# Projections of 128 tokens over 512 columns in one pass, with queries kept unscaled in DRAM

## The chip, the cores and the metric

The kernel runs on one core of one Trainium2 chip. The metric is the device time of one execution in microseconds (us). The kernel before takes 1717.66 us, the median of three runs that lie between 1717.14 and 1718.26 us.

Engine names in what follows: PE is TensorE (matrix products, also transposes), DVE is VectorE, ACT is ScalarE, POOL is GpSimd, SP is SyncE, whose queue issues every DMA transfer here. Each engine runs its instructions in the order in which they stand in its own queue.

## The reference

One layer of a decoder on 1024 tokens of width 1024, all in float32. Cut to what matters here:

```python
xn = rms_norm(x, norm_mix)
proj = xn @ w_in
q_nsa, kv_nsa, g_nsa, conv_in, q_mem, g_merge = split(proj, [512, 768, 24, 1024, 512, 3072])
# A: sparse attention, 8 heads of 64 in 2 groups
q = rms_norm(heads(q_nsa), nsa_qk_norm[0])
k_c, v_c, k_s, v_s, k_w, v_w = split(kv_nsa, 6)       # compressed, selected, window
ks, kw = rms_norm(k_s, nsa_qk_norm[2]), rms_norm(k_w, nsa_qk_norm[3])
br_nsa = nsa_attention(q, kc, vc, ks, vs, kw, vw, sigmoid(g_nsa)) @ w_nsa_out
# B: gated convolution of width 31 per channel, LayerNorm over the 512 channels, silu
a, ag = split(conv_in, 2)
br_conv = silu(layer_norm(causal_conv31(a * sigmoid(ag)) + conv_b)) @ w_conv_out
# C: cross attention, 4 heads of 128, into 256 memory tokens
qm = rms_norm(heads(q_mem), mem_qk_norm[0]); km = rms_norm(..., mem_qk_norm[1])
br_mem = (softmax(qm @ km.T * 128 ** -0.5) @ vm) @ w_mem_out
# merge and feed forward
gm = sigmoid(g_merge)
h = x + (gm[0] * br_nsa + gm[1] * br_conv + gm[2] * br_mem) @ w_out
out = h + (silu(hn @ w_gate) * (hn @ w_up)) @ w_down     # hn = rms_norm(h, norm_ffn)
```

## The kernel before

**Products.** A float32 factor is split into a high part, which PE takes in a fast 32-bit format, and the rest (`split`, line 130: a cast on ACT, a subtraction on DVE). A product is then three matmuls, high by high, high by low, low by high (`mm3`, line 151). Almost all work of PE goes through `mm` at line 144.

**Normalised tokens.** `norm_x` (line 246) takes 256 tokens of x at a time. ACT squares and sums each row (L204), takes the root (L136), DVE inverts it and scales the row (L208), PE transposes it in 128x128 pieces (L229), ACT scales the pieces by the gain into the high part (L220), DVE makes the low part (L221). Both halves of the 1024 tokens stay in SBUF as eight tiles (`XN`).

**Projections that are laid out by token** (`tok_proj`, line 279) make 128 tokens by 256 columns in one PSUM bank half: 8 steps of depth times 3 matmuls of 256 columns; two such tiles fill a bank. Their weights come as two loads of 512 rows by 256 columns (`row_units`, line 269). They are run for the queries of the cross attention (columns from `C_QM`, two passes), the queries of the sparse attention (from `C_Q`, two passes), and the selected and window keys and values (from `C_KV`, two passes), besides four passes over the memory tokens. `raw_proj` (line 324) copies queries from PSUM to SBUF; `head_norms` (line 308) later squares, sums, scales them in place. The queries stay in four SBUF tiles (`QMQ[0]`, `QMQ[1]`, `Q[0]`, `Q[1]`).

**Order of the program:** x is normalised along with the first pass of cross-attention queries (lines 337 to 346); then the convolution's input projections, gates, compressed keys and values, memory keys and values; then cross attention (`mem_attention`, line 569) for two pairs of heads, each along a further pass of queries; the last pass of queries; the tail of the convolution (lines 613 to 635: two sums over channels by `ones` matmuls, square, root, reciprocal, silu); the keys and values (lines 638 to 662); then sparse attention.

**Taps.** The 31 taps of the convolution for four channel tiles, 124 DVE instructions of about 1.3 us (lines 373, 374), are spread by hand over the products between the first projection and the last query (lines 598 to 605).

**Sparse attention** is a list of 80 units: for each of 8 token tiles and each of 2 groups one compressed, two selected and two window units. `scores(u)` runs four units ahead of `values(u)`. I call the five units of one token tile and group a group of units; each begins with a transpose of the queries at line 688.

**Filler.** The merge gates' projection (line 801 on) has 24 weight tiles, each with two halves of 24 matmuls of 512 columns. It has the lowest priority (`FILL`) and its own single PSUM bank `pf`; each half ends in an ACT copy (L814) to `fz` and a DMA to `zd`. The scheduler puts it wherever it expects PE to have nothing else. The first 12 tiles (`N_EARLY`), 24 halves, may stand anywhere; each step of the later ones must stand behind a certain unit of the attention.

**What sets the order.** A scheduler orders the instructions of each engine once, before the run, by priority and by when it expects their inputs. On the chip the order is fixed.

## Time and profile before

| | |
|---|---|
| median of three runs | 1717.66 us |
| the profiled execution, its own time | 1716.36 us |
| span of its trace | 1714.6 us |
| PE busy | 1692.3 us (99% of the span) |
| DVE busy | 1065.6 us (62%) |
| ACT busy | 731.3 us (43%) |
| POOL busy | 515.2 us (30%) |
| mean granted TensorE clock | 0.999 |

The stages lie in the trace thus: the first queries and the normalisation of x to 57 us, the convolution's projections and compressed keys to 190 us, memory tokens and cross attention to 370 us, queries, keys and the convolution's tail to 443 us, sparse attention to 850 us, then branch projections, merge and feed forward. "Busy" says that a matmul was somewhere in PE, not that PE ran at its peak: how close it is, the distance from one matmul's start to the next one's tells.

### The profile page before, as it was taken

How to read it: one execution, taken by the hardware profiler on the slowest of the kernel's cores; microseconds unless marked ns; L12 is line 12 of the kernel's file. 1: busy time of each engine (PE TensorE's matmuls, PEld its weight loads, DVE VectorE, ACT ScalarE, POOL GpSimd, SP SyncE). 2: the span in 40 equal slices, each digit the busy share in tenths (PEclk: the TensorE clock that was granted, in tenths of full speed). 3: DMA queues.
4: the chain of work that ended last, by engine and by line, in shares of the span. 5: the costliest groups of instructions: out<-in, count | busy, mean ns of one | idle time of the engine just before them, and what ended most of it. 6: DMA issues, size and time to landing. Idle time of an engine off the chain costs nothing.

```text
span 1714.6 us, 24413 instructions
## 1 busy us (share of the span) xinstructions
PE 1692.3 (99%) x9096; PEld 1457.9 (85%) x9096; DVE 1065.6 (62%) x1825; ACT 731.3 (43%) x1370; POOL 515.2 (30%) x478
## 2 busy tenths in 40 slices
PE   7999999999999999999999999999999999999999
PEld 7887998999888889999888888788888888888887
DVE  5599997876355566666654625856545554466665
ACT  6312544444466656666653424533222222233332
POOL 0000011200145434444204501375555777310000
PEclk9999999999999999999999999999999999999999
DMA  6112433112122111111385223233333445793763
GB/s 213 50 40 74 160 93 99 38 56 75 50 67 64 57 38 56 47 34 45 127 290 197 98 80 117 77 113 106 110 99 123 145 163 166 270 393 135 224 236 123
DMA packets 174173, 203.51 MB, mean 119 GB/s; under 512 B 10772, under 2 KB 117572, under 8 KB 173030
## 3 DMA queue, kind: packets, MB, share of 16 engines
q1 hardware_dynamic: 174054, 201.95, 35.4%
q8 instruction: 71, 1.16, 0.3%
q14 instruction: 48, 0.39, 0.1%
HBM read 151.58 MB, written 50.33 MB: 118 GB/s over the span
## 4 chain that ended last, share of the span: by engine, by line
PE 93%; DVE 3%; ACT 2%; issue 1%; DMA 1%; POOL 0%; SPq 0%; DVEq 0%; ACTq 0%; POOLq 0%
PE ps L144 57%; PE pf L144 19%; PE ps L1158 11%; PE ps L762 3%; PE pf L1158 1%; DVE slab L132 1%; PE ps L688 0%; PE ps L229 0%; PE ps L746 0%; DMA st<-in_w_in_dram 0%; PE ps L552 0%; DVE wsl L132 0%; ACT slab L131 0%; ACT slab L220 0%; DVE t L128 0%
## 5 line engine op out<-in xcount | busy, mean ns | idle before, releaser
L144 PE MATMUL ps<-slab,wsl 128*128 128x512 f32 (+1 forms) x1664 | 370.3, 381 | 1.4 <-ACT slab L131 0.9
L144 PEld LDWEIGHTS ps<-slab,wsl 128*128 128x128 f32 x1664 | 301.9, 188 | 61.5 <-ACT slab L131 1.2
L144 PE MATMUL pf<-slab,fsl 128*128 128x512 f32 x1236 | 323.1, 399 | 4.2 <-ACT fz L814 1.7
L144 PEld LDWEIGHTS pf<-slab,fsl 128*128 128x128 f32 x1236 | 222.9, 188 | 45.7 <-ACT fz L814 3.1
L144 PE MATMUL ps<-wsl,slab 128*128 128x256 f32 (+1 forms) x1512 | 221.1, 299 | 3.5 <-ACT slab L220 1.5
L144 PEld LDWEIGHTS ps<-wsl,slab 128*128 128x128 f32 x1512 | 199.5, 192 | 14.7 <-DVE slab L221 3.3
L1054 DVE TENSOR_TENSOR t<-ps,t 128x512 f32<-128x512 f32 x127 | 86.9, 688 | 108.0 <-PE ps L144 106.8
L374 DVE SCALAR_TENSOR_TENSOR slab<-slab,cw 128x1021 f32<-128x1021 f32 (+16 forms) x120 | 151.6, 1270 | 1.7
L144 PE MATMUL ps<-slab,fsl 128*128 128x512 f32 x636 | 147.8, 389 | 0.0
L144 PEld LDWEIGHTS ps<-slab,fsl 128*128 128x128 f32 x636 | 119.4, 188 | 24.9
L132 DVE TENSOR_TENSOR t<-ps,t 128x512 fp32r<-128x512 f32 (+2 forms) x192 | 117.2, 630 | 25.5 <-ACT t L131 23.9
L1158 PE MATMUL ps<-wsl 128*128 128x512 f32 x495 | 118.5, 389 | 0.0
L144 PE MATMUL ps<-t,slab 128*128 128x256 f32 x624 | 115.3, 292 | 0.9 <-DVE t L132 0.8
L132 DVE TENSOR_TENSOR wsl<-st,wsl 128x1024 fp32r<-128x1024 f32 x64 | 83.0, 1297 | 50.6 <-ACT wsl L131 47.5
L542 POOL TENSOR_SCALAR t<-t,sm 128x256 f32<-128x256 f32 x32 | 25.4, 810 | 286.2 <-DVE sm L538 286.2
L1158 PEld LDWEIGHTS ps<-wsl 128*128 128x128 f32 x495 | 92.9, 188 | 19.3
L131 ACT CAST wsl<-st 128x1024 fp32r<-128x1024 f32 x65 | 68.3, 1051 | 91.8 <-PE ps L144 50.6
L131 ACT CAST t<-ps 128x512 fp32r<-128x512 f32 (+2 forms) x192 | 97.5, 539 | 20.2 <-PE ps L762 18.4
L144 PEld LDWEIGHTS ps<-t,slab 128*128 128x128 f32 x624 | 93.6, 189 | 6.3 <-DVE t L132 1.0
L144 PE MATMUL ps<-slab,qt 128*128 128x384 f32 (+3 forms) x384 | 94.7, 338 | 0.0
L131 ACT CAST wsl<-t 128x1024 fp32r<-128x1024 f32 x42 | 44.2, 1054 | 97.6 <-POOL t L128 43.3
L676 POOL TENSOR_SCALAR wsl<-wsl,sm,gsb 128x640 f32<-128x640 f32 (+7 forms) x76 | 59.7, 795 | 77.7 <-DVE sm L671 67.2
(238 smaller groups left out, 2698.4 us busy)
## 6 DMA issues: line engine op xcount, KB each, us to landing
t<-in_w_down_dram SPq DMA_DIRECT2D x70, 256.0 KB, 4.2
fst<-in_w_in_dram SPq DMA_DIRECT2D x24, 512.0 KB, 3.6
zd<-fz SPq DMA_DIRECT2D x48, 256.0 KB, 2.0
t<-zd SPq DMA_DIRECT2D x24, 512.0 KB, 4.0
st<-in_w_in_dram SPq DMA_DIRECT2D x22, 512.0 KB, 3.6
st<-in_w_gate_dram SPq DMA_DIRECT2D x22, 512.0 KB, 4.4
st<-in_w_up_dram SPq DMA_DIRECT2D x22, 512.0 KB, 4.1
ad<-t SPq DMA_DIRECT2D x44, 256.0 KB, 3.3
```

The source lines that it names most:

```text
L131: m = nc.scalar.copy(hi, src)
L132: return m, (eng or nc.vector).tensor_tensor(lo, src, hi.bitcast(F32), op=OP.subtract)
L144: m = nc.tensor.matmul(o, a, b, start=start, stop=stop)
L374: return nc.vector.scalar_tensor_tensor(acc[:, s:], u[:, :S - s], cw[:, ct, 30 - s:31 - s], acc[:, s:], op0=OP.mult, op1=OP.add)
L542: nc.gpsimd.tensor_scalar(pm[:, tt, h, :], pm[:, tt, h, :], rec[:, j:j + 1], 1.0, op0=OP.mult, op1=OP.mult)
L676: nc.gpsimd.tensor_scalar(tiles[h], tiles[h], rec[:, h:h + 1], gsb[:, i, c0:c0 + 1], op0=OP.mult, op1=OP.mult)
L762: nc.tensor.transpose(b[:, j - j0, h, :], tiles[h][:, j * P:(j + 1) * P], ident)
L1054: nc.vector.tensor_tensor(o, a_, b_, op=OP.add)
L1158: nc.tensor.matmul(B[t], a_, b_, start=start and k == 0 and j == 0, stop=k == FH - 1 and j == 2, skip_group_check=True)
```

## The change

1. Queries, selected and window keys and values are projected 512 columns at a time (`wide_proj`, `wide_unit`): 128 tokens in one PSUM bank, weights as four loads of 256 rows by 512 columns.
2. All four heads of cross-attention queries are now made in the first stage, and all sparse-attention queries along the two rounds of cross attention; the keys and values follow.
3. Queries are copied from PSUM and sent to a DRAM buffer `qraw` as they are; only their sums of squares stay (`rqm`, `rqn`). `mem_qT` and `load_q` read them back and scale them.
4. The keys stand ahead of the code that spreads the taps, so that the taps are spread over the keys too, and the tail of the convolution comes behind the keys.

```diff
+    def wide_unit(w, c0, u, st=None, alloc=wslab):
+        if st is None:
+            st = stage.tile([P, 2, 512], F32, tag="st", name=nm("st"))
+        nc.sync.dma_start(st, w[u * 256:(u + 1) * 256, c0:c0 + 512].rearrange("(k p) c -> p k c", p=P))
...
+        split(w_[0], w_[1], st)
+        return w_
+    def wide_proj(ws, t):
+        o = bank([512])
+        half, a = t // 4, (t % 4) * P
+        for k in range(KT):
+            hi, lo = ws[k // 2]
+            mm3(o, xn(0, k, half, a, a + P), xn(1, k, half, a, a + P), hi[:, k % 2, :], lo[:, k % 2, :], k == 0, k == KT - 1)
+        return o
+    def queries(ws, t, j, stat):
+        h = stat.shape[2]
+        ps = wide_proj(ws, t)
+        raw, sq = t2([512]), t2([h, 512 // h])
+        nc.scalar.copy(raw, ps)
+        nc.sync.dma_start(qraw[j, t], raw)
+        nc.scalar.activation(sq, ps.rearrange("p (h d) -> p h d", h=h), AF.Square)
+        nc.vector.tensor_reduce(stat[:, t, :], sq, axis=AX.X, op=OP.add)
...
-    ws = row_units(w_in, C_QM)
+    ws = [wide_unit(w_in, C_QM, u, alloc=slab) for u in range(2)]
     xin += [rows2(x, tp * 256) for tp in range(1, 4)]
+    norm_x(0)
+    ws += [wide_unit(w_in, C_QM, u, t4([2, 512]), slab) for u in range(2, 4)]
...
+    for t in range(NT):
+        queries(ws, t, 0, rqm)
+        if t % 2 == 0 and t < NT - 2:
+            norm_x(t // 2 + 1)
+    stat_rms(rqm)
...
     def mem_qT(hp, tp):
-        qn = QMQ[hp][:, 2 * tp:2 * tp + 2]
+        qn = t2([2, 2, P])
+        nc.sync.dma_start(qn.rearrange("p t h d -> p t (h d)"),
+                          qraw[0, 2 * tp:2 * tp + 2, :, hp * 256:(hp + 1) * 256].rearrange("t p c -> p t c"))
+        nc.vector.tensor_tensor(qn, qn, rqm[...].to_broadcast([P, 2, 2, P]), op=OP.mult)
+        gain_mul(qn, gm[:, 0, :])
...
-                raw_proj(ws, tp, dest)
+                queries(ws, 4 * hp + tp, 1, rqn)
...
+    ws = [wide_unit(w_in, C_Q, u, alloc=slab if u == 3 else wslab) for u in range(4)]
+    mem_attention(0, ws)
+    pm3 = mem_attention(1, ws)
+    stat_rms(rqn)
+    KSW = [slab([2, S]) for _ in range(2)]
+    VSW = [slab([NT, 2, P]) for _ in range(2)]
+    ws = [wide_unit(w_in, C_KV, u, alloc=t4 if u == 3 else wslab) for u in range(4)]
...
+    for t in range(NT):
+        v = wide_proj(ws, t).rearrange("p (s a g d) -> p s a g d", s=2, a=2, g=2)
...
     with low(TAP):
         along = products[first_tap:]
...
+    def load_q(i):
+        QN[i] = t2([8, 64])
+        nc.sync.dma_start(QN[i].rearrange("p h d -> p (h d)"), qraw[1, i])
+        nc.vector.tensor_tensor(QN[i], QN[i], rqn[:, i, :, None].to_broadcast([P, 8, 64]), op=OP.mult)
```

**Where instructions stand now, on two engines' queues.** Of two names joined by an arrow the left is written; `slab_140` and `slab_143` are tokens 0 to 255 of x, `slab_159` and `slab_162` tokens 256 to 511, `ps` a PSUM bank, `pf` the filler's, `wsl`, `fsl` and `st` weights.

ACT in the first stage of the kernel before, from the first high parts of x on:

```order
L220 ACTIVATE slab_169<-ps_189,gcol 128x256
L220 ACTIVATE slab_170<-ps_198,gcol 128x256
L204 ACTIVATE t_31_252,sm_251<-slab_159 128x1024
L220 ACTIVATE slab_171<-ps_207,gcol 128x256
L220 ACTIVATE slab_172<-ps_216,gcol 128x256
L136 ACTIVATE sm_254<-sm_251 128x1
L220 ACTIVATE slab_169<-ps_189,gcol 128x256
L220 ACTIVATE slab_170<-ps_198,gcol 128x256
L204 ACTIVATE t_35_260,sm_259<-slab_159 128x1024
```

ACT in the same place of the changed kernel, from the last high part of the first 256 tokens on:

```order
L223 ACTIVATE slab_174<-ps_218,gcol 128x256
L131 CAST fsl_7127<-fst_7125 128x1024
L322 COPY t_33_263<-ps_238 128x512
L324 ACTIVATE t_34_264<-ps_238 128x512
L207 ACTIVATE t_36_270,sm_269<-slab_162 128x1024
L131 CAST wsl_669<-st_667 128x1024
L136 ACTIVATE sm_272<-sm_269 128x1
L131 CAST wsl_674<-st_672 128x1024
L207 ACTIVATE t_40_278,sm_277<-slab_162 128x1024
L131 CAST fsl_7188<-fst_7186 128x1024
L136 ACTIVATE sm_280<-sm_277 128x1
L131 CAST wsl_786<-st_784 128x1024
```

The squares of tokens 256 to 511 stood among the high parts of tokens 0 to 255; now they stand behind the copy and the square of the first product `ps_238`, with casts of the convolution's weights between them.

PE in the first stage of the changed kernel, from the end of the first product on:

```order
L144 MATMUL ps_238<-slab_234,slab_174 128x512 x6
L232 MATMUL ps_285<-ident,slab_162 128x128
L232 MATMUL ps_294<-ident,slab_162 128x128
L232 MATMUL ps_303<-ident,slab_162 128x128
L232 MATMUL ps_312<-ident,slab_162 128x128
L144 MATMUL ps_321<-slab_154,slab_171 128x512 x6
L144 MATMUL ps_321<-slab_159,slab_172 128x512 x6
L144 MATMUL ps_321<-slab_229,slab_173 128x512 x6
```

Transposes of token tile 2 stand between the products of token tiles 0 and 1, as they did before with products of half the width.

PE at the convolution's tail in the kernel before (`ones` marks the sums over channels):

```order
L144 MATMUL ps_3148<-slab_640,ones 128x512
L144 MATMUL ps_3154<-slab_640,ones 128x512
L144 MATMUL ps_3209<-wsl_3201,slab_169 128x256 x6
L144 MATMUL ps_3209<-wsl_3201,slab_170 128x256 x6
L144 MATMUL pf_7939<-slab_172,fsl_7936 128x512 x2
L144 MATMUL ps_3209<-wsl_3206,slab_171 128x256
L144 MATMUL pf_7939<-slab_172,fsl_7936 128x512 x2
```

PE at the same place in the changed kernel:

```order
L144 MATMUL ps_3218<-slab_677,ones 128x512
L144 MATMUL pf_7679<-slab_171,fsl_7676 128x512 x6
L144 MATMUL pf_7679<-slab_172,fsl_7676 128x512 x6
L144 MATMUL pf_7679<-slab_173,fsl_7676 128x512 x6
L144 MATMUL pf_7679<-slab_174,fsl_7676 128x512 x6
L144 MATMUL pf_7707<-slab_383,fsl_7676 128x512 x6
L144 MATMUL pf_7707<-slab_384,fsl_7676 128x512 x6
L144 MATMUL pf_7707<-slab_385,fsl_7676 128x512 x6
L144 MATMUL pf_7707<-slab_386,fsl_7676 128x512 x6
L144 MATMUL ps_3231<-slab_677,ones 128x512
```

Beside the tail there stood projections of keys with a little filler; now there is filler alone. In all, 336 filler matmuls (14 halves) stood ahead of the first transpose of the sparse attention, and 528 (22 halves) stand there now; at the twelfth group of units it is 906 in both.

## Rows read from the trace of the kernel before

**Rows 1.** The page: span, busy times, the chain that ended last by engine

```profile
span 1714.6 us, 24413 instructions
...
PE 1692.3 (99%) x9096; PEld 1457.9 (85%) x9096; DVE 1065.6 (62%) x1825; ACT 731.3 (43%) x1370; POOL 515.2 (30%) x478
...
PE 93%; DVE 3%; ACT 2%; issue 1%; DMA 1%; POOL 0%; SPq 0%; DVEq 0%; ACTq 0%; POOLq 0%
```

**Rows 2.** PE's timeline: start, length, line, tiles, count; 512 columns, then 256

```profile
65.42 78.74 PE L144 MATMUL ps<-slab,wsl 128*128 128x512 f32 x346
144.00 7.51 PE L144 MATMUL ps<-slab,t 128*56 128x512 f32 x32
...
240.41 8.56 PE L144 MATMUL ps<-wsl,slab 128*128 128x256 f32 x70
248.80 1.04 PE L552 MATMUL ps<-ident,t 128*128 128x128 f32 x8
```

**Rows 3.** PE's groups to 56.56 us: count, busy, mean ns, idle before

```profile
L144 PE MATMUL ps<-wsl,slab 128*128 128x256 f32 x192 | 29.6, 300 | 2.3 <-ACT slab L220 1.5 <-DVE slab L221 0.4
L229 PE MATMUL ps<-ident,slab 128*128 128x128 f32 x64 | 10.5, 320 | 0.7 <-DVE slab L208 0.7
L144 PE MATMUL pf<-slab,fsl 128*128 128x512 f32 x28 | 8.1, 402 | 1.0 <-ACT fsl L131 0.7 <-DVE fsl L132 0.3
L144 PE MATMUL ps<-slab,wsl 128*128 128x512 f32 x16 | 4.0, 391 | 0.0
```

**Rows 4.** ACT's timeline in the first stage

```profile
9.02 1.05 ACT L131 CAST wsl<-st 128x1024 fp32r<-128x1024 f32 x1 [0.39 <-DMA st<-in_w_in_dram]
9.97 0.83 ACT L220 ACTIVATE slab<-ps,gcol 128x256 fp32r<-128x256 f32 x2
10.69 1.05 ACT L204 ACTIVATE t<-slab 128x1024 bf16<-128x1024 f32 x1
11.64 0.20 ACT L204 ACTIVATION_READ_ACCUMULATOR t<-slab 128x1 f32 x1
...
12.45 0.21 ACT L136 ACTIVATE sm<-sm 128x1 f32<-128x1 f32 x1
...
24.18 0.62 ACT L326 COPY slab<-ps 128x512 f32<-128x512 f32 x1
```

**Rows 5.** DVE's timeline in the first stage

```profile
8.66 1.23 DVE L132 TENSOR_TENSOR wsl<-st,wsl 128x1024 fp32r<-128x1024 f32 x1 [0.64 <-ACT wsl L131]
...
11.24 1.87 DVE L221 SCALAR_TENSOR_TENSOR slab<-ps,gcol,slab 128x256 fp32r<-128x256 f32 x4
13.03 0.15 DVE L138 RECIPROCAL sm<-sm 128x1 f32<-128x1 f32 x1
...
13.48 0.75 DVE L208 TENSOR_SCALAR slab<-slab,sm 128x1024 f32<-128x1024 f32 x1
```

**Rows 6.** Stretches: PE, PEld, DVE, ACT, POOL busy (count), granted clock, DMA share, GB/s

```profile
10.00:12.00 2.00, 1.56 (x8) 1.22 (x6) 1.90 (x3) 2.00 (x6) 0.00 (x0) 1.00 1.03 414
12.00:14.00 2.00, 1.04 (x6) 0.68 (x6) 1.87 (x6) 2.00 (x6) 0.00 (x0) 1.00 1.02 410
14.00:16.00 2.00, 1.92 (x13) 1.72 (x12) 1.76 (x6) 1.24 (x5) 0.00 (x0) 0.72 1.02 401
16.00:18.00 2.00, 2.00 (x11) 2.00 (x11) 0.55 (x1) 0.00 (x0) 0.00 (x0) 0.50 1.10 286
18.00:20.00 2.00, 2.00 (x18) 2.00 (x17) 0.00 (x0) 0.00 (x0) 0.00 (x0) 0.93 1.19 298
```

**Rows 7.** DVE's lines in the convolution's tail: ns min/median/max, first and last start

```profile
L619 DVE TENSOR_TENSOR slab<-slab,ps x8: 680/682/689, 372.8 to 378.1; 128x512 f32<-128x512 f32 x8
...
L630 DVE RECIPROCAL t<-t x2: 3294/3319/3344, 390.0 to 393.3; 128x512 f32<-128x512 f32 x2
...
L632 DVE TENSOR_TENSOR slab<-slab,t x8: 675/684/686, 396.8 to 401.0; 128x512 f32<-128x512 f32 x8
```

**Rows 8.** PE's timeline where one filler half follows another

```profile
293.37 0.96 PE L144 MATMUL pf<-slab,fsl 128*128 128x512 f32 x3 [0.67 <-ACT fz L814]
```

**Rows 9.** Stretches as in rows 6: groups 1 to 11, 4, 14

```profile
442.95:689.88 246.93, 246.35 (x1484) 218.03 (x1484) 135.13 (x488) 150.19 (x406) 108.04 (x149) 1.00 0.18 57
497.94:516.75 18.81, 18.81 (x117) 16.60 (x115) 10.55 (x45) 12.76 (x39) 10.54 (x16) 1.00 0.22 67
744.84:773.69 28.85, 28.85 (x192) 26.45 (x191) 18.98 (x61) 19.29 (x44) 12.30 (x14) 1.00 0.14 42
```

**Rows 10.** PE's groups in 442.95 to 689.88 us: the filler

```profile
L144 PE MATMUL pf<-slab,fsl 128*128 128x512 f32 x570 | 150.1, 399 | 0.0
```

**Rows 11.** Group 3 of the attention: DVE ends the queries' split, PE uses it

```profile
482.12 0.69 DVE L132 TENSOR_TENSOR qt<-ps,qt 128x512 fp32r<-128x512 f32 x1 [0.55 <-ACT qt L131]
...
486.30 0.19 PE L144 MATMUL ps<-kcmp,qt 128*128 128x64 f32 x1
```

More of the change, by code (lines that the diff above doesn't have):

```diff
@@ L193, in hybrid_layer_kernel @@
     md = drp.tile([4, P, S], F32, tag="md", name="md")
+    qraw = drp.tile([2, NT, P, 512], F32, tag="qraw", name="qraw")
     gcol = const([2 * KT], F32, "gcol")
@@ L580, in mem_attention, with keys @@
         return pm[3]
[L582 to L595 removed]
+    ws = [wide_unit(w_in, C_Q, u, alloc=slab if u == 3 else wslab) for u in range(4)]
[5 more added lines that the diff above has]
+    ws = [wide_unit(w_in, C_KV, u, alloc=t4 if u == 3 else wslab) for u in range(4)]
+    def keys(t, cat):
+        b = bank([2, 2, P], F32R)
+        for j in range(4):
+            nc.tensor.transpose(b[:, j // 2, j % 2, :], cat[:, j].rearrange("p a d -> p (a d)"), identr)
+        for s in range(2):
+            nc.vector.tensor_copy(KSW[s][:, :, t * P:(t + 1) * P], b[:, s].bitcast(F32))
+    last = None
+    for t in range(NT):
+        v = wide_proj(ws, t).rearrange("p (s a g d) -> p s a g d", s=2, a=2, g=2)
+        if t == 0:
+            mem_out(1, 3, pm3, products[-1][0])
+        kn = t2([2, 2, 64])
+        heads_norm(v[:, :, 0], kn)
+        nc.vector.tensor_tensor(kn, kn, gn[:, 2:4, None, :].to_broadcast([P, 2, 2, 64]), op=OP.mult)
+        cat = t2([4, 2, 64], F32R)
+        split(cat[:, :, 0, :], cat[:, :, 1, :], kn.rearrange("p s g d -> p (s g) d"))
+        for s in range(2):
+            split(VSW[s][:, t, :, 0:64], VSW[s][:, t, :, 64:128], v[:, s, 1])
+        if last is not None:
+            keys(t - 1, last)
+        last = cat
+    keys(NT - 1, last)
     with low(TAP):
```

83 lines of the change are left out of this document (20 added, 63 removed).

## The prediction

> **What bounds the kernel now.** I read the page's shares first: of the chain that ended last 93% is PE, and PE is busy for 99% of the span [rows 1]. "Busy" is not "at its peak", so the timeline comes next: in a closed row of projections 346 matmuls of 512 columns stand from 65.42 to 144.00 us and 70 of 256 columns from 240.41 to 248.80 us [rows 2]. The distances are 78.58 / 346 = 227.1 ns and 8.39 / 70 = 119.9 ns: 0.444 and 0.468 ns per column. So PE sets the time nearly throughout, a matmul taken away is a gain at its distance, and an idle moment of PE is a loss in full. A second look by stretches shows where that isn't so: at the start, where PE waits for ACT and DVE and its matmuls take 300 ns and more of busy time in the mean [rows 3].
>
> The sum is made on the profiled execution, 1716.36 us (span 1714.6 and 1.8 around it); the median of the runs lies 1.3 us higher, and that is added at the end. This kernel can be told from no change at about 0.2%, 3.4 us.
>
> **1. Projections, a gain of 7.3 us.** Queries and keys were 4 x 2 x 3 passes of 48 matmuls of 256 columns, 1152 in all; they become 576 of 512 columns. 1152 x 0.1199 = 138.1 us against 576 x 0.2271 = 130.8 us. A stretch with longer distances than 119.9 is not ruled out, but since a matmul of 256 columns can't cost more than it does with PE closed, I let the gain lie between 7 and 10.
>
> The Trainium skill (TensorE: Matmul & The Clock Gate, section "Back-to-back issue gap") gives a lone matmul's gap at the full clock as columns / 2.4 GHz plus 2.5 ns. By it two passes of 256 cost only 2.5 ns more than one of 512, 1.4 us for the 576 pairs, and the sum would be 6 us later. The trace disagrees (2 x 119.9 - 227.1 = 12.7 ns per pair), and its number is taken.
>
> **2. The start, a loss of 11 us.** Before, PE had finished by 56.56 us 192 matmuls of 256 columns (23.0 us at the distance above), 64 transposes (0.13 each by the last of [rows 2], 8.3) and 44 matmuls of 512 columns (10.0) [rows 3]. That is 41.3 us of work, so 15.3 were lost. For the changed kernel I follow the three queues with durations from the rows.
>
> First product. One pass of 512 columns needs four weight units, each with a cast on ACT and a low part on DVE, while PE's first product needs all of them. On ACT four high parts (0.41 each, from 9.97) end at 11.6, and two casts (1.05) at 13.7 [rows 4]. On DVE the first four low parts end at 13.1 (11.24 + 1.87), two low parts of weights (1.23 each) at 15.6, and the first low part of the second four at 16.1 [rows 5]. From there 21 matmuls remain, 4.8 us, with about 1 more for a low clock: 21.8 us. PE has then done 24 matmuls (5.4) and 16 transposes (2.1): 14.3 lost, nearly what was lost in all before.
>
> Then PE idles. Its next instructions are the transposes of token tile 2. Their squares now stand on ACT behind the copy and the square of that first product, with the casts of the convolution's weights between. From the end of the product: copy 0.62, square about the same, row sum 1.05 + 0.20, cast 1.05, root 0.21 [rows 4], reciprocal 0.15, scaling 0.75 with at most one low part of 1.23 ahead of it on DVE [rows 5], and a second cast 1.05 when the weights are in time. That is 4.7 to 6.9; I take 6.7, since the order has the casts ahead of the root and the transfers that feed them (512 KB at 400 GB/s, 1.3 us each [rows 6]) should have landed by 25 us. Were their squares free to go first, as before, nothing of this would be lost.
>
> The clock. In the rows by stretch the granted clock is 1.00 while PE is busy 1.56 and 1.04 of 2 us, and afterwards, with PE full, 0.72, 0.50 (1.2 of 2.4 GHz) and 0.93 [rows 6]: 2 x (0.28 + 0.50 + 0.07) = 1.7 us lost after a thin stretch. I expect the same once more after the idle time: 1.7. Token tile 3 has its root and scaling behind a filler's copy (0.62 + 0.21 + 0.15 + 0.75 = 1.7), and the high and low parts of both tiles hold their products by some 2. Together 14.3 + 6.7 + 1.7 + 1.7 + 2 = 26.4 lost against 15.3: 11. Bounds: 4 (the idle time of 6.7 alone, less what the later products give back) and 14 (a second such gap before the next 256 tokens).
>
> **3. The convolution's tail, a loss of 2 us.** Its chain on DVE, from the first subtraction at 372.8 us to the last product at 401.7 [rows 7], had projections of keys beside it; subtractions, reciprocals and products alone are 8 x 0.68 + 2 x 3.32 + 8 x 0.68 = 17.5 us, with adds, squares and roots and two scalings of queries some 25. In the new order the keys are done, and beside the tail stands filler alone: 133 matmuls between the last sum and the first use by the attention, 133 x 0.227 = 30 us. So the chain is costed at nothing; were that cover missing, it would cost up to 25. But filler has a single bank. Where one half follows another PE waited 0.67 us for ACT's copy [rows 8]. The order has four to six such places with nothing between, against two: 2 to 4 times 0.67, and with the copies delayed behind ACT's other work up to 4. I take 2, keep 0 and 4.
>
> **4. The attention has less filler, a loss of 5 us.** Ahead of its first transpose stand 528 filler matmuls, formerly 336; at the twelfth group both have the same number. The 192 are moved, not added. Groups 1 to 11 had 246.9 us, PE busy 246.35 [rows 9], with 570 filler matmuls [rows 10]; now 378, so 43.6 us less of PE's work. If PE stays fed, these groups take 203.3 us and nothing is lost. Other engines then come closer: POOL 108 and DVE 135 of 203 us, ACT 150 less the copies of eight halves (8 x 0.62 = 5), 145, 71%. Group 14 already runs at ACT 19.29 and DVE 18.98 of 28.85 us, 67 and 66%, without an idle moment of PE. Group 4 has 18 filler matmuls fewer by the order; it goes from 18.81 to 18.81 - 18 x 0.227 = 14.7 us with ACT at some 12.0, 82%, which no row shows to hold. In group 3 the queries' low part is done at 483.17 (482.12 + 0.69), and PE takes the queries at 486.30 [rows 11]: some 3 us of slack, and 18 fewer filler matmuls take 4.1 of it. Bounds: 0, and 27, where the first six groups keep their old pace (120 matmuls fewer in them, 27 us). By group 14 I am nearer to 0, and take 1 us for each of five groups.
>
> **5. Costed at nothing.** Sixteen writes and as many reads of 256 KB for `qraw`: the DMA share is 0.18 in the attention [rows 9], a read has a product of 48 matmuls and more between itself and its use, and each query is scaled once as before. Transposes, copies of keys and splits keep their number. The spread of the taps over the keys takes DVE's load off the earlier products, and with PE at 99% there is little to gain from it; without that cover DVE's 17.5 us of the tail would be late, counted in 3.
>
> **Sum.** -7.3 + 11 + 2 + 5 = +10.7: 1716.4 + 10.7 = 1727.1, and with 1.3 for the median 1728.
>
> **The rivals.**
> *Only the projections count.* The early stage is fed, since the lists of casts are served while PE still works on the first product, and both tail and attention hide as before: 1717.7 - 7.3 = 1710. For it: DVE is relieved of taps, and 22 us of idle PE in the whole trace are mostly at the start and stay. Against it: PE's next row there is a transpose that can't start before the product's copy has left ACT. Chance 0.11.
> *A draw.* The start costs 4 to 7, tail and attention 0 to 2: 1714.2 to 1721.1, middle 1717. For it: every loss in 3 and 4 is at places where PE was never idle before. Chance 0.23.
> *The attention starves.* Scores need queries, whose scaling, doubling on POOL, transpose and split are a chain over four engines, and filler stood beside it. From the point where this chain and a group's softmax take longer than PE's 12 to 17 us, filler that was used up early is missing: -7.3 + 11 + 2 + 27 = +33, 1750. For it: ACT at 82% in group 4. Against it: group 14. Chance 0.11.
> *The change doesn't do what it says*: the scheduler might have kept the old pairs of products. The order shows rows of 128x512 for the queries, so I give that no chance of its own.
>
> **How the numbers follow.** The forecast has 1721 to 1738 and 0.55; the draw 0.23; faster 0.11; starved 0.11. Slower by over 0.2% is 0.55 + 0.11 = 0.66, the same 0.23, faster 0.11. The range leaves out the faster rival's lower part and the starved attention's upper part: 1713 to 1742.
>
> **What would show it.** Right: PE idle for some 6 us at 21 to 28 us ahead of the transposes at the place of L229, waited for by DVE's scaling; a granted clock under 1 just behind it; waits for `fz` between filler halves at the tail; groups 1 to 11 in 203 to 210 us; rows of 128x512 at 227 ns for queries and keys. Wrong: no idle time over 3 us after the first product (then term 2 is too large by as much), a tail that PE waits for by more than 4 us, or idle PE before the scores in the first six groups.

## The result, and the profile of the changed kernel

The changed kernel takes 1728.85 us (median of 4 runs, 1728.06 to 1729.47); the kernel before, run on the same chip, 1717.40. The ratio is 1.0066 with a 95% interval of 1.0049 to 1.0084: slower by 11.5 us. Its profiled execution has a span of 1727.5 us against 1714.6 [rows 1], 12.9 us more, and the rows below place that difference. One run of a kernel of the experiments further down (e13_held, 9118.71 us where its other four took 1724.84 to 1728.58) is left out of its median.

The page of the changed kernel, its span and busy times:

```profile
span 1727.5 us, 23330 instructions
...
PE 1693.1 (98%) x8520; PEld 1428.3 (83%) x8520; DVE 1070.3 (62%) x1839; ACT 726.9 (42%) x1371; POOL 515.7 (30%) x478
```

PE has 576 instructions fewer and is "busy" for 0.8 us more: the saving of the projections doesn't show in this line. A matmul counts as busy from its start to its end, 381 ns in the mean for 512 columns on the page of either kernel, while in a closed row the next one starts after 227 ns: so part of a longer distance, be it from a wait or from half the clock, is counted as busy time.

To place the difference I add up, over all PE instructions of a stretch, the distance from one's start to the next one's, less the median distance of that width in both traces (227, 176, 120, 109 and 111 ns for 512, 384, 256, 128 and 64 columns). I call this PE's excess. It contains waits, low clock and small gaps alike, and is zero for a closed row. What is left, the work at its own pace, is 1676.4 us before and 1668.9 after.

| stage | excess before, us | after, us | difference |
|---|---|---|---|
| to 75 us, with the time to PE's first instruction | 17.0 | 27.5 | +10.5 |
| 75 us to the first `ones` matmul (371.7; 458.3) | 5.2 | 3.3 | -1.9 |
| the tail, to the attention (443.0; 489.0) | 2.4 | 3.7 | +1.3 |
| attention, groups 1 to 3 | 1.6 | 6.8 | +5.2 |
| attention, groups 4 to 11 | 2.0 | 6.7 | +4.7 |
| groups 12 to 16, to 870 us | 2.7 | 3.2 | +0.5 |
| from 870 us on | 3.5 | 3.5 | 0.0 |
| PE's work at its own pace | 1676.4 | 1668.9 | -7.5 |

The sum is +12.8 us. One trace of each kernel stands behind it, of an execution within 1.1 us of the kernel's median; the traces of e12_all (1714.35 us) and e13_held (1724.84) are of executions 2.5 and 2.2 us below theirs. Where a kernel of the experiments below shares a stage with the changed one, the stage's excess came out within 1.5 us of it.

**The start.** PE's timeline, its waits and the rows after them (start, length, line, tiles, count, idle time before and who ended it):

```profile
15.36 7.37 PE L144 MATMUL ps<-slab,slab 128*128 128x512 f32 x19 [0.85 <-DVE slab L224]
29.09 1.12 PE L232 MATMUL ps<-ident,slab 128*128 128x128 f32 x4 [6.36 <-DVE slab L211]
29.86 7.44 PE L144 MATMUL ps<-slab,slab 128*128 128x512 f32 x21
...
51.98 0.66 PE L232 MATMUL ps<-ident,slab 128*128 128x128 f32 x4 [1.76 <-DVE slab L211]
```

The first product of 512 columns ends at 22.73 us, PE stands still for 6.36 us, and the 21 matmuls behind take 37.13 - 29.86 = 7.27 us where 21 x 0.227 = 4.77 would do. ACT's timeline in the idle time shows what the transposes wait for:

```profile
22.77 0.59 ACT L322 COPY t<-ps 128x512 f32<-128x512 f32 x1 [6.45 <-PE ps L144]
23.25 0.60 ACT L324 ACTIVATE t<-ps 128x512 f32<-128x512 f32 x1
23.74 1.06 ACT L207 ACTIVATE t<-slab 128x1024 bf16<-128x1024 f32 x1
24.68 0.20 ACT L207 ACTIVATION_READ_ACCUMULATOR t<-slab 128x1 f32 x1
24.77 1.04 ACT L131 CAST wsl<-st 128x1024 fp32r<-128x1024 f32 x1
25.71 0.21 ACT L136 ACTIVATE sm<-sm 128x1 f32<-128x1 f32 x1
26.07 1.04 ACT L131 CAST wsl<-st 128x1024 fp32r<-128x1024 f32 x1
```

ACT was idle for 6.45 us while PE worked, because its next instruction was the copy of that product; then came, one behind another, copy, square, the squares of tokens 256 to 383, a weight cast and the root. On DVE the reciprocal and then a weight's low part of 1.23 us stood ahead of the scaling:

```profile
26.99 0.16 DVE L138 RECIPROCAL sm<-sm 128x1 f32<-128x1 f32 x1
27.14 1.23 DVE L132 TENSOR_TENSOR wsl<-st,wsl 128x1024 fp32r<-128x1024 f32 x1
28.29 0.75 DVE L211 TENSOR_SCALAR slab<-slab,sm 128x1024 f32<-128x1024 f32 x1
```

The stretches of the same time, columns as in [rows 6]; the first figure after the POOL column is the granted clock:

```profile
22.00:24.00 2.00, 0.73 (x4) 0.27 (x2) 0.12 (x1) 1.24 (x3) 0.00 (x0) 1.00 1.13 344
24.00:26.00 2.00, 0.00 (x0) 0.00 (x0) 0.72 (x2) 1.92 (x4) 0.00 (x0) 0.69 1.13 339
26.00:28.00 2.00, 0.00 (x0) 0.00 (x0) 2.00 (x3) 1.94 (x3) 0.00 (x0) 0.50 0.56 195
28.00:30.00 2.00, 0.91 (x5) 0.91 (x5) 1.90 (x3) 1.20 (x4) 0.00 (x0) 0.50 0.89 227
30.00:32.00 2.00, 2.00 (x6) 1.61 (x6) 1.32 (x4) 1.05 (x1) 0.00 (x0) 0.50 1.06 272
32.00:34.00 2.00, 2.00 (x6) 1.52 (x6) 1.09 (x1) 0.00 (x0) 0.00 (x0) 0.50 0.91 252
34.00:36.00 2.00, 2.00 (x9) 1.59 (x8) 0.00 (x0) 0.00 (x0) 0.00 (x0) 0.75 0.91 243
```

PE reads as fully busy from 30 to 34 us, with 6 matmuls in 2 us: its granted clock is 0.50 there, which is 1.2 of 2.4 GHz.

**The projections.** PE's timeline in the first stage; the next row starts at 85.64 us, so 26 matmuls of 512 columns stand 5.89 / 26 = 226.5 ns apart, as in [rows 2]:

```profile
79.75 6.05 PE L144 MATMUL ps<-slab,slab 128*128 128x512 f32 x26
85.64 4.47 PE L144 MATMUL ps<-slab,wsl 128*128 128x512 f32 x19
```

**The attention.** The stretch of groups 1 to 11, and in it who held PE up (waiting engine and tile, releaser, us in all, times, longest; this second view ends at 652.4 us):

```profile
489.00:701.30 212.30, 205.93 (x1283) 180.88 (x1282) 133.00 (x486) 146.65 (x396) 107.28 (x147) 1.00 0.20 63
```

```profile
PE ps L144 <- DVE t L132: 2.4, 5, 0.6
PE ps L711 <- POOL t L707: 1.7, 3, 0.7
PE pf L144 <- ACT fz L838: 1.1, 2, 0.8
```

PE is idle for 6.4 us where it was for 0.6 [rows 9], in many short waits, by DVE, POOL and ACT in turn, none over 0.8 us. The engines that it waits for have no more work than before in these groups (ACT 146.65 against 150.19 us, DVE 133.0 against 135.1), but 212.3 us for it instead of 246.9: ACT is busy for 69% of them instead of 61%. The excess of these groups, 13.5 us, is more than the idle time; the rest lies in distances that grew without showing as idle.

### The profile page after: what moved, and what is told of

Same layout as the page of the kernel before. It is cut to its first block, busy times and chain, and to the rows that moved or that the text cites. A ratio compares the mean times of both kernels' runs of the same rounds, so it can differ in the third digit from the quotient of the medians.

```text
span 1727.5 us, 23330 instructions
## 1 busy us (share of the span) xinstructions
PE 1693.1 (98%) x8520; PEld 1428.3 (83%) x8520; DVE 1070.3 (62%) x1839; ACT 726.9 (42%) x1371; POOL 515.7 (30%) x478
## 4 chain that ended last, share of the span: by engine, by line
PE 65%; DVE 3%; ACT 1%; issue 1%; POOL 0%; DMA 0%; ACTq 0%; DVEq 0%; POOLq 0%
PE ps L144 39%; PE pf L144 11%; PE ps L1182 11%; PE ps L785 3%; PE pf L1182 1%; DVE slab L132 1%; DVE t L132 1%; PE ps L769 0%; DVE t L128 0%; DVE wsl L753 0%; DVE slab L753 0%; PE ps L711 0%; ACT slab L131 0%; DMA t<-in_x_dram 0%; ACT wsl L757 0%
## 5 line engine op out<-in xcount | busy, mean ns | idle before, releaser
L393 DVE SCALAR_TENSOR_TENSOR slab<-slab,cw 128x1023 f32<-128x1023 f32 (+14 forms) x120 | 152.1, 1268 | 2.0
L144 PE MATMUL ps<-wsl,slab 128*128 128x512 f32 (+1 forms) x648 | 140.2, 360 | 0.3 <-DVE slab L224 0.3
L144 PE MATMUL ps<-t,slab 128*128 128x256 f32 (+1 forms) x672 | 128.5, 299 | 1.7 <-DVE t L132 1.3
L144 PEld LDWEIGHTS ps<-wsl,slab 128*128 128x128 f32 x648 | 108.1, 189 | 17.7 <-DVE slab L224 0.5
L144 PE MATMUL ps<-slab,slab 128*128 128x512 f32 x468 | 119.6, 406 | 2.7 <-ACT slab L223 1.8
L144 PEld LDWEIGHTS ps<-t,slab 128*128 128x128 f32 x672 | 103.0, 189 | 10.4 <-DVE t L132 2.1
L144 PEld LDWEIGHTS ps<-slab,slab 128*128 128x128 f32 x468 | 91.0, 197 | 23.8 <-ACT slab L223 2.6
L132 DVE TENSOR_TENSOR wsl<-st,wsl 128x1024 fp32r<-128x1024 f32 x58 | 75.4, 1300 | 46.3 <-ACT wsl L131 45.1
L131 ACT CAST wsl<-st 128x1024 fp32r<-128x1024 f32 x59 | 62.0, 1050 | 81.6 <-PE ps L144 41.0
```

What stands on the lines that cost most here:

```text
L131: m = nc.scalar.copy(hi, src)
L132: return m, (eng or nc.vector).tensor_tensor(lo, src, hi.bitcast(F32), op=OP.subtract)
L144: m = nc.tensor.matmul(o, a, b, start=start, stop=stop)
L393: return nc.vector.scalar_tensor_tensor(acc[:, s:], u[:, :S - s], cw[:, ct, 30 - s:31 - s], acc[:, s:], op0=OP.mult, op1=OP.add)
```

## The experiments

Eleven kernels were run. Times are medians; "excess" is that of the table above, taken from each kernel's own trace.

| kernel | us | ratio to before (95%) | to 75 us | mid | tail | groups 1-3 | 4-11 | 12-16 |
|---|---|---|---|---|---|---|---|---|
| before | 1716.5 to 1717.4 | 1 | 11.1 | 5.2 | 2.4 | 1.6 | 2.0 | 2.7 |
| after | 1728.85 | 1.0066 (1.0049 to 1.0084) | 21.8 | 3.3 | 3.7 | 6.8 | 6.7 | 3.2 |
| e1_norm_first | 1716.50 | 0.9999 (0.9990 to 1.0009) | 10.0 | 3.7 | 3.7 | 6.8 | 6.5 | 3.3 |
| e3_tail_first | 1722.47 | 1.0035 (1.0022 to 1.0048) | 20.3 | 3.2 | 4.0 | 0.8 | 7.4 | 2.9 |
| e4_early8 | 1761.10 | 1.0259 (1.0244 to 1.0274) | 20.8 | 3.5 | 27.4 | 14.4 | 3.5 | 1.2 |
| e5_load_later | 1725.62 | 1.0051 (1.0035 to 1.0068) | 20.7 | 3.3 | 3.7 | 4.6 | 7.1 | 2.1 |
| e9_early16 | 1728.35 | 1.0070 (1.0053 to 1.0087) | 21.2 | 3.4 | 3.7 | 2.7 | 5.8 | 6.9 |
| e10_norm_tail | 1713.53 | 0.9988 (0.9978 to 0.9997) | 9.2 | 5.9 | 3.9 | 0.8 | 7.4 | 2.6 |
| e11_queries_sbuf | 1713.58 | 0.9985 (0.9975 to 0.9994) | 10.1 | 4.8 | 4.2 | 0.4 | 7.6 | 3.2 |
| e12_all | 1716.87 | 0.9997 (0.9987 to 1.0006) | 8.8 | 5.9 | 3.8 | 1.2 | 3.0 | 7.8 |
| e13_held | 1727.07 | 1.0058 (1.0044 to 1.0071) | 8.5 | 12.6 | 10.3 | 4.8 | 1.9 | 2.9 |
| e14_held_tail_behind | 1723.45 | 1.0037 (1.0024 to 1.0050) | 8.6 | 14.6 | 3.7 | 2.8 | 6.5 | 3.3 |
| e15_taps_early | 1709.69 | 0.9961 (0.9947 to 0.9975) | 9.9 | 2.4 | 3.7 | 1.9 | 5.2 | 2.6 |

In this table the time to PE's first instruction (5.6 to 6.0 us) is left out of the column "to 75 us".

### Is it ACT's order that stops PE at the start?

```diff
         ps = wide_proj(ws, t)
+        if between is not None:
+            between()
         raw, sq = t2([512]), t2([h, 512 // h])
...
-        queries(ws, t, 0, rqm)
-        if t % 2 == 0 and t < NT - 2:
-            norm_x(t // 2 + 1)
+        queries(ws, t, 0, rqm, (lambda: norm_x(t // 2 + 1)) if t % 2 == 0 and t < NT - 2 else None)
```

> The changed kernel with the normalisation of the next 256 tokens written between a product of the first stage and that product's copy, as the kernel before had it; nothing else differs. Theory S (the squares' place in ACT's queue, behind the copy and square of the first product and casts of the convolution's weights, makes PE idle 6.4 us at 22.7 to 29.1 us and the low clock after it): PE's wait ahead of those transposes falls under 1 us, PE's excess over its own pace in the first 75 us falls from 21.8 to some 13 us, and the time from 1728.9 to 1718 to 1721. Rival W (the weights and x arrive too late whatever ACT's order, the transfers being at 400 GB/s): 4 us or more of the wait stay, the time stays over 1725.

It took 1716.50 us, 12.3 less than the change; the gain is larger than I had expected. PE's timeline at the place where it stood still:

```profile
15.67 7.32 PE L144 MATMUL ps<-slab,slab 128*128 128x512 f32 x19 [1.04 <-DVE slab L224]
22.83 0.60 PE L232 MATMUL ps<-ident,slab 128*128 128x128 f32 x4
23.19 1.41 PE L144 MATMUL ps<-slab,slab 128*128 128x512 f32 x5
```

No wait is left at 22.83 us. ACT did the squares at 17.17 and 18.47 us, in time that it had spent waiting for the copy. The second stretch of low clock went with it, as the granted clock of e1_norm_first shows (the 1.00 in these rows):

```profile
22.00:24.00 2.00, 2.00 (x13) 1.65 (x12) 0.00 (x0) 0.97 (x2) 0.00 (x0) 1.00 1.13 350
24.00:26.00 2.00, 2.00 (x17) 1.82 (x16) 0.69 (x1) 1.15 (x3) 0.00 (x0) 1.00 1.11 322
```

So the excess to 75 us fell from 21.8 to 10.0, a little under that of the kernel before (11.1). Rival W falls: weights and x are there. All other columns of the table stayed within 0.4 us of the change's. The granted clock below 1.00 ahead of the first product's end, from 14 to 22 us, is in both kernels (rows of 2 us: 0.63, 0.50, 0.50, 0.67 in the changed one, 0.67, 0.50, 0.50, 0.63 in e1_norm_first).

### Filler or buffers in the attention?

Two theories could explain the attention's 10 us: its first groups lack filler, or its buffers run short. In the pool `t2` of six buffers two are now held by queries, and in the trace of the change POOL's doubling of the queries for group 3 starts when DVE has read another such buffer:

```profile
517.13 0.85 DVE L799 TENSOR_TENSOR t<-ps,t 64x256 f32<-64x256 f32 x2 [1.39 <-ACT t L796]
```

```profile
518.12 1.27 POOL L707 TENSOR_TENSOR t<-t,gn 128x512 f32<-128x512 f32 x1 [1.44 <-issue]
519.66 0.45 POOL L692 TENSOR_SCALAR wsl<-wsl,sm,gsb 128x128 f32<-128x128 f32 x1 [0.27 <-DVE sm L687]
```

```diff
-N_EARLY = 12
+N_EARLY = 8
```

> The changed kernel with 8 instead of 12 tiles of the filler free to stand anywhere. By its order 384 filler matmuls (formerly 528) stand ahead of the attention's first transpose, none beside the convolution's tail, and groups 1 to 11 have 480 instead of 378. Theory F (the 10 us by which PE's excess in groups 1 to 11 grew come from missing filler): that excess falls from 13.5 to 4 to 8 us; the tail has lost its filler, and the first groups wait instead, 2 to 8 us; the time 1722 to 1732. Rival B (they come from the six buffers of the pool t2, two of which now hold queries): the excess in groups 4 to 11 stays as it is, 7 to 8 us.

```diff
-            if g == 0 and i + 1 < NT:
+            if g == 1 and i + 1 < NT:
                 load_q(i + 1)
```

> The changed kernel with the queries of the next token tile loaded and scaled in the second group of a tile instead of the first, so that they hold a buffer of the pool t2 half as long. Rival B (buffers): POOL's doubling of the queries no longer comes late, PE's waits for it (1.7 us in three places) go, and groups 1 to 11 get 2 to 4 us shorter: 1725 to 1727. Theory F (missing filler): nothing over 1 us, 1728 to 1730; should the load come too late for the next tile, PE waits at the first group of a tile for it and the time rises by up to 5 us.

e4_early8 was far slower than either theory allowed, 1761.1 us, and groups 1 to 11 lost 17.9 us, not 4 to 8. What it showed first was the price of the cover at the tail. PE's waits between 449 and 480 us:

```profile
455.38 0.72 PE L619 MATMUL ps<-identr,t 128*128 128x128 f32 x4 [4.68 <-DVE t L132]
...
465.25 3.75 PE L144 MATMUL ps<-slab,ones 128*128 128x512 f32 x4 [7.32 <-DVE slab L654]
...
479.25 1.12 PE L711 MATMUL ps<-ident,t 128*128 128x128 f32 x4 [10.24 <-POOL t L707]
```

The tail's excess rose from 3.7 to 27.4 us: uncovered, the chain costs 23.7 us, low clock included. Groups 1 to 3, with 72 filler matmuls instead of 99, lost another 7.6, and the work from 870 us on lost 7.3. The 7.6 us don't measure the missing filler alone: 12.9 of the 14.4 us are lost in group 1, which has 3 filler matmuls and begins right behind the waits of the tail, and the granted clock was 0.50 until 498 us:

```profile
454.00:479.25 25.25, 6.31 (x10) 2.19 (x11) 19.30 (x22) 7.07 (x10) 1.59 (x1) 0.50 0.07 21
479.25:498.00 18.75, 11.68 (x46) 9.75 (x46) 7.38 (x37) 12.04 (x33) 6.17 (x13) 0.50 0.28 113
```

But groups 4 to 11, with 360 instead of 279, fell from 6.7 to 3.5, which rival B had said they wouldn't.

e5_load_later took 1725.62 us, 3.2 less than the change and in the range of rival B. Groups 1 to 3 fell from 6.8 to 4.6, groups 4 to 11 did not (6.7, 7.1); the other 2 us lie at the start and in groups 12 to 16. So buffers have a part, about 2 us in the first three groups, but no more.

### Does it help to give the attention its filler back from its own end?

```diff
-N_EARLY = 12
+N_EARLY = 16
```

> The changed kernel with 16 instead of 12 tiles of the filler free to stand anywhere; nothing else. By its order the same 528 filler matmuls stand ahead of the attention, but groups 1 to 7 have 70, 50, 48, 48, 48, 48, 45 as before the change (now 48, 24, 27, 30, 33, 30, 33), and the last nine 24 to 30. Theory F (the attention's loss is missing filler in its first groups): PE's excess in groups 1 to 11 falls from 13.5 to 3 to 6 us with none new behind, 1719 to 1723. Rival B (buffers of t2 or the queries' way over DRAM): the excess stays over 9 us and the time over 1725.

It did not: 1728.35 us, the same as the change. The excess moved with the filler, 6.8 to 2.7 in groups 1 to 3, 6.7 to 5.8 in groups 4 to 11, and up from 3.2 to 6.9 in groups 12 to 16, which now have 162 filler matmuls instead of 246:

```profile
714.90:870.00 155.10, 151.61 (x1010) 137.77 (x1008) 115.71 (x344) 110.85 (x238) 61.28 (x70) 1.00 0.19 63
```

PE is idle there for 3.5 us; in the change it was for 1.1 (701.30 to 870.00 us, PE busy 167.57). In groups 2 to 7, which got 45 to 50 filler matmuls instead of 24 to 33, the excess of each, 0.8 to 3.2 us before, is 0.1 to 0.7; in groups 8 to 11, which have 24 to 27 instead of 33 to 42, it rose from 2.5 to 5.2 us together. So theory F was right that a group loses time where it lacks filler. It was wrong in "none new behind" and in the size: groups 1 to 11 kept 8.5 us, not 3 to 6, and rival B's time (over 1725) came true though its reason did not. There is a fixed stock, and what counts is how much of it is gone before the attention begins.

### What takes filler ahead of the attention?

e3_tail_first moves the block from the line with `low(TAP)` to the last `ud` transfer in one piece from behind the keys to ahead of them.

```diff
+    with low(TAP):
+        along = products[first_tap:]
...
     KSW = [slab([2, S]) for _ in range(2)]
     VSW = [slab([NT, 2, P]) for _ in range(2)]
```

> The changed kernel with the spread of the taps and the tail of the convolution written ahead of the keys again (part 4 of the change undone). By its order the keys' products stand beside the tail, and 480 instead of 528 filler matmuls stand ahead of the attention. Theory F: PE's excess at the tail and in groups 1 and 2 falls by 2 to 4 us, the relief of DVE before (1.9 us between 75 us and the tail) is given back: 1726 to 1729. Rival T (the tail's place behind the keys costs the attention its filler and so most of its 10 us): 1722 or less.

It took 1722.47 us, between the two expectations. Groups 1 to 3 have 147 filler matmuls instead of 99, and their excess fell from 6.8 to 0.8; nothing else in the table moved by more than 1.5 us. The relief of DVE before the tail, which I expected to be given back, was not: 3.2 against 3.3. So the 1.9 us that the change gains between 75 us and the tail do not come from spreading the taps over the keys.

> The two edits of e1_norm_first and e3_tail_first together: the normalisation between product and copy, the convolution's tail ahead of the keys. If their gains are of separate stages they add: 1728.9 - 12.3 - 6.4 = 1710, from 1708.5 to 1712; if both only shift the same idle time, 1714 or more.

Both edits together took 1713.53 us, between the two expectations: 15.3 less than the change where the single gains add to 18.7. The start and groups 1 to 3 kept theirs (9.2; 0.8); some 2.5 us came back between 75 us and the tail, where one wait of 2.24 us for the filler's bank stands at 279.90 us. With an interval of 0.9978 to 0.9997 this is a little faster than the kernel before.

e11_queries_sbuf keeps the sparse attention's queries on the chip, in two tiles `QK`:

```diff
-        QN[i] = t2([8, 64])
-        nc.sync.dma_start(QN[i].rearrange("p h d -> p (h d)"), qraw[1, i])
+        QN[i] = QK[i // 4][:, i % 4].rearrange("p (h d) -> p h d", h=8)
```

> e10_norm_tail with the queries of the sparse attention kept in two SBUF tiles instead of DRAM: no write, no read, no buffer of t2 for them (the cross attention's queries still go over DRAM, and one weight unit stands in another pool). My costing (the way over DRAM is free): within 1.5 us of e10_norm_tail. Rival D (the reads and the buffers that they hold cost the attention): 2.5 to 5 us less than e10_norm_tail, mostly as shorter groups 4 to 11.

1713.58 against 1713.53 us: the way over DRAM and the buffers that it takes, for the sparse attention's eight writes and eight reads, cost nothing that can be measured here (the two intervals against the kernel before overlap almost wholly), and groups 4 to 11 are as they were (7.6, 7.4). With enough filler in groups 1 to 3 the 2 us of e5_load_later are gone as well.

e12_all is e10_norm_tail with the edit of e5_load_later and `N_EARLY = 16`.

> e10_norm_tail with the queries loaded one group later (as in e5_load_later) and 16 free tiles of filler (as in e9_early16): groups 1 to 9 have 48 and more filler matmuls, the last seven 27 to 30. Theory F: 1703 to 1707, PE's excess in groups 1 to 11 at 2 to 5 us, below the kernel before by the 7.5 us of the projections and more. Should the last groups now wait for their missing filler, 1708 to 1712, with the excess in groups 12 to 16.

1716.87 us, over both expectations. In its trace groups 4 to 11 fell to 3.0 and groups 12 to 16 rose to 7.8: e9_early16 once more. The trace is of one of its faster executions (1714.35 us), so where the other 2.5 us of the median go isn't shown.

### Can filler simply be held back?

```diff
     pm3 = mem_attention(1, ws)
+    crossed = products[-1][0]
...
                     first = mm3(ps, w[:, 0, k, :], w[:, 1, k, :], xn(0, k, h_), xn(1, k, h_), k == 0, k == KT - 1)
+                    if h_ == 0 and k == 0 and n_ == 6:
+                        tc.add_manual_dep(first.ins, crossed.name, ORDER, reason="held until cross attention is done")
```

> e10_norm_tail with the seventh and later tiles of the filler held behind the last product of queries in the cross attention. By its order 288 instead of 381 filler matmuls stand ahead of the tail, 360 instead of 480 ahead of the attention, and its groups have 48, 58, 38, 48, 48, 72, 48 and so on, 546 instead of 426 in groups 1 to 11. Theory F (the scheduler spent filler in the cross attention where PE would not have waited): the excess of groups 1 to 11 falls from 8.2 to 2 to 5 us, the cross attention gains no wait over 2 us, 1707 to 1711. Rival C (the cross attention needs that filler as much as the attention): its excess between 75 us and the tail rises by 4 us or more and the time stays at 1713 or above.

> e1_norm_first with the same hold; the tail stays behind the keys as in the change. By its order 456 instead of 528 filler matmuls stand ahead of the attention, and groups 1 to 5 have 68, 51, 45, 28, 42 instead of 48, 24, 27, 30, 33. Theory F: the excess of groups 1 to 11 falls from 13.3 to 6 to 9 us, 1710 to 1714. Rival C: the stretch from 75 us to the tail loses what the attention gains, 1716 or above.

No: 1727.07 and 1723.45 us, 13.5 and 7.0 more than the kernels without the hold. Groups 4 to 11 of e13_held have 402 filler matmuls, as the kernel before, and an excess of 1.9, as the kernel before had 2.0. But the stretch from 75 us to the tail rose from 5.9 to 12.6 and the tail from 3.9 to 10.3. Who held PE up in e13_held between 280 and 480 us:

```profile
PE ps L144 <- DVE t L132: 6.4, 3, 5.5
PE ps L144 <- DVE sm L754: 2.3, 1, 2.3
PE ps L540 <- DVE t L346: 1.0, 2, 0.7
```

Rival C was right: in this order the cross attention waits for DVE when it has no filler. In e14_held_tail_behind groups 1 to 3 got 4.0 us back, and the stretch from 75 us to the tail lost 10.9. At the longest wait of e13_held DVE was busy with the convolution's tail: eight of its subtractions (L634) and a weight's low part stood ahead of the low part that PE needed.

```profile
375.94 2.47 DVE L634 TENSOR_TENSOR slab<-slab,ps 128x512 f32<-128x512 f32 x4
378.32 1.22 DVE L132 TENSOR_TENSOR wsl<-st,wsl 128x1024 fp32r<-128x1024 f32 x1
379.46 2.47 DVE L634 TENSOR_TENSOR slab<-slab,ps 128x512 f32<-128x512 f32 x4
381.85 0.68 DVE L132 TENSOR_TENSOR t<-ps,t 128x512 fp32r<-128x512 f32 x1
```

In the second half of its cross attention the kernel before has as little filler, 23 matmuls against 24 in e13_held, and there its excess is 0.0 us against 16.0 (both counted from the middle one of the transposes of its probabilities to the last). So the lack of filler alone doesn't make the wait. Whether the tail's place on DVE makes it, the taps', or the scaling of the queries that are now read back there, these runs don't separate.

### Does the late start of the taps spend the filler?

DVE's line of the taps, 120 of its 124 instructions, first and last start, in the kernel before and in the changed one:

```profile
L374 DVE SCALAR_TENSOR_TENSOR slab<-slab,cw x120: 1156/1266/1486, 79.2 to 349.3; 128x1023 f32<-128x1023 f32 x4, 128x1022 f32<-128x1022 f32 x4, 128x1021 f32<-128x1021 f32 x4, 128x1020 f32<-128x1020 f32 x4
```

```profile
L393 DVE SCALAR_TENSOR_TENSOR slab<-slab,cw x120: 1234/1265/1367, 113.7 to 427.4; 128x1023 f32<-128x1023 f32 x4, 128x1022 f32<-128x1022 f32 x4, 128x1021 f32<-128x1021 f32 x4, 128x1020 f32<-128x1020 f32 x4
```

The taps begin 34.5 us later. They need the convolution's first channel tile. Ahead of the first tap PE has now all eight products of cross-attention queries at full width (192 matmuls of 512 columns instead of 256, 20.6 us more), the start's 10.5 us, and 17 filler matmuls more (3.9 us). In the meantime DVE has little to do: from 57 to 112 us it was busy for 43.07 us in the kernel before and is for 15.15 us in the changed one (one row of each):

```profile
57.00:112.00 55.00, 55.00 (x246) 45.29 (x245) 43.07 (x46) 12.86 (x16) 0.00 (x0) 1.00 0.19 50
```

```profile
57.00:112.00 55.00, 54.89 (x257) 44.86 (x257) 15.15 (x32) 18.16 (x38) 0.26 (x2) 1.00 0.11 36
```

So DVE has 28 us less work behind it at 112 us. But the cross attention begins later too: its first transpose of probabilities stands at 248.8 us in the kernel before and at 287.5 in the changed one, and 86 and 79 of these taps have begun by then; ten stand behind its last one now, where none did. And e1_norm_first had moved the first tap forward by 13.9 us already:

```profile
L393 DVE SCALAR_TENSOR_TENSOR slab<-slab,cw x120: 1236/1265/1366, 99.8 to 415.9; 128x1023 f32<-128x1023 f32 x4, 128x1022 f32<-128x1022 f32 x4, 128x1021 f32<-128x1021 f32 x4, 128x1020 f32<-128x1020 f32 x4
```

It gave no filler back: 528 filler matmuls stand ahead of its attention, as in the change, and groups 1 to 11 lose the same. The taps' lead over the cross attention, which begins at 275.9 us there, is 176 us, and the change had not shortened it (170 us in the kernel before, 174 in the changed one). So the late first tap by itself doesn't explain the filler. To give the taps a longer lead, four of the eight products were put behind the first channel tile, on top of e10_norm_tail (the last 256 tokens are normalised one product earlier for it):

```diff
-    for t in range(NT):
-        queries(ws, t, 0, rqm, (lambda: norm_x(t // 2 + 1)) if t % 2 == 0 and t < NT - 2 else None)
-    stat_rms(rqm)
+    norms = {0: 1, 2: 2, 3: 3}
+    for t in range(4):
+        queries(ws, t, 0, rqm, (lambda: norm_x(norms[t])) if t in norms else None)
+    wqm = ws
...
         first_tap = first_tap or len(products)
+        if ct == 0:
+            for t in range(4, NT):
+                queries(wqm, t, 0, rqm)
+            stat_rms(rqm)
```

> e10_norm_tail with only four of the eight products of cross-attention queries in the first stage (the other four behind the convolution's first channel tile), so that the first tap, at 99 us in e10_norm_tail and 79 us in the kernel before, can start some 20 us earlier. Theory T (the late start of 124 taps on DVE stretches everything ahead of the attention, and the scheduler fills PE's time there with filler that the attention then lacks): the order has 333 instead of 381 filler matmuls ahead of the tail and 432 instead of 480 ahead of the attention, groups 3 to 5 have 48, 48, 42 instead of 27, 30, 33; the first tap stands at 77 to 85 us, no new wait comes in the cross attention (excess between 75 us and the tail 4 to 8 us), the excess of groups 1 to 11 falls from 8.2 to 4 to 6 us, 1709 to 1712. Rival C (the cross attention needs the filler, as when it was held back): that excess rises by 4 us or more, 1714 or above.

It took 1709.69 us, in the range of theory T, 0.9961 of the kernel before (0.9947 to 0.9975) and the fastest kernel here. The taps and DVE's busy time from 57 to 112 us:

```profile
L394 DVE SCALAR_TENSOR_TENSOR slab<-slab,cw x120: 1143/1267/1491, 74.9 to 341.0; 128x1023 f32<-128x1023 f32 x4, 128x1022 f32<-128x1022 f32 x4, 128x1021 f32<-128x1021 f32 x4, 128x1020 f32<-128x1020 f32 x4
```

```profile
57.00:112.00 55.00, 55.00 (x244) 45.56 (x243) 39.06 (x36) 11.88 (x17) 0.26 (x2) 1.00 0.12 39
```

With 432 instead of 480 filler matmuls ahead of the attention no wait came into the cross attention. But the gain lies elsewhere than theory T had put it: between 75 us and the tail, where nothing was to change, the excess fell from 5.9 to 2.4 (the wait of 2.24 us of e10_norm_tail is gone), and in groups 1 to 11 only from 8.2 to 7.1, where 4 to 6 were expected. So the time agrees in part by luck. And the edit moved two things, the taps and 96 matmuls of queries; which of them gave the 48 filler matmuls back is not separated. The taps' lead over the cross attention (271.9 us) is 197 us here, 186 in e10_norm_tail.

## Why the prediction was right, step by step

The forecast was 1728 us and the result is 1728.85; the sum was +10.7 and the profile shows +12.8. It is right in sign and size, in part by luck: the attention lost 5.4 us more than forecast, and a gain of 1.9 us that was not forecast, with 1.4 us less from the other three terms together, took 3.3 of them back.

**Term 1, projections** (-7.3): the work at PE's own pace fell by 7.5 us, 576 times 2 x 120 - 227 = 13 ns. The term follows the trace, whose closed row above has 226.5 ns between matmuls of 512 columns. By the Trainium skill (TensorE: Matmul & The Clock Gate, section "Back-to-back issue gap") the gap of a lone one would be 215.8 ns at the full clock, an estimate from its formula; the trace doesn't agree. The reason that the prediction gives for its bound of 7 us, that 256 columns can't cost more than with PE closed, is shown by no row; the bound held all the same.

**Term 2, the start** (+11): +10.5. The idle time was 6.36 us (6.7 forecast), at the place and with the releaser that had been named, and e1_norm_first shows that ACT's order is its cause. The low clock behind it was put at 1.7 and cost 2.5 (7.27 against 4.77 us). The first product ended at 22.73 us, 0.9 later than forecast; its own low clock, put at 1, cost 3.4 by the granted clock of 0.63, 0.50, 0.50 and 0.67 in the rows of 2 us from 14 to 22. The later tiles were put at 1.7 + 2 and show one wait of 1.76 us. One reading of [rows 3] misleads: a mean of 300 ns for 256 columns is no sign of a slow start, since the page of the whole execution has 299.

**Term 3, the tail** (+2): +1.3, and waits of 0.68 and 0.72 us for `fz` stand where halves meet, the size of [rows 8]. That the chain was costed at nothing because of its cover is shown by e4_early8: without cover it costs 23.7 us, "up to 25" by the prediction.

**Term 4, the attention** (+5): +9.9 in groups 1 to 11, and +0.5 behind. The step that failed is the one that took 1 us each for five groups "by group 14". Groups 1 to 11 took 212.3 us, outside the 203 to 210 named as a sign of being right, and two of PE's three waits for POOL's doubling of the queries, 1.0 us together ahead of groups 3 and 4, are the idle time before the scores named as a sign of being wrong. Group 14 ran closed with 45 filler matmuls and more work of its own, so it was no model for groups with 24 to 36; in the changed kernel each of the first nine groups has an excess of 0.6 to 3.2 us, most for group 2 with 24 filler matmuls, and only groups 10 and 11 run closed (0.1, 0.2). (A sum of the prediction is off here: 482.12 + 0.69 is 482.81, not 483.17, so the slack in group 3 was 3.5 us and not 3.1; 18 filler matmuls, 4.1 us, exceed it either way.) What groups 4 to 11 lose follows, by and large, the filler that they have:

| filler matmuls in groups 4 to 11 | excess, us | kernels |
|---|---|---|
| 279, 286 | 6.5 to 7.6 | after, e1, e3, e5, e10, e11; e14 |
| 294, 306 | 5.8, 5.2 | e9, e15 |
| 342, 360 | 3.0, 3.5 | e12, e4 |
| 402 | 1.9, 2.0 | e13, before |

**Not forecast:** the 1.9 us gained between 75 us and the tail. The kernel before has three waits there, 1.04, 0.68 and 0.67 us; the changed one has two, of 0.26 and 0.68 us. e3_tail_first rules out the spread over the keys as their cause; what it is stays open.

**Right for a reason that was incomplete:** the prediction read from the order that 528 filler matmuls stand ahead of the attention instead of 336, and called them moved. Why the program spends them, it did not ask, and the runs answer that in part. Of the 192 the tail's place behind the keys accounts for 48 (e3_tail_first has 480), and the products ahead of the convolution, with the late taps, for another 48 (e15_taps_early has 432). The other 96 still stand ahead of the attention there, most of them in the cross attention: between the first and the last transpose of its probabilities the kernel before has 149 filler matmuls, the changed one 225 and e15_taps_early 240. What puts them there stays open. Costed at nothing were the queries over DRAM (e11_queries_sbuf: right for the sparse attention's half; the other half was not tested) and the taps' spread (no gain seen: right).

The rivals: the draw's start (4 to 7) and the faster rival's (0) fall with the 10.5 us; the starved attention's 27 us fall with the 9.9, which is twice the forecast's 5 and about a third of the rival's.
